# Layer 1's first feed-forward product by seven quarter products in a two-layer attention trunk

## The chip, the cores and the metric

The kernel runs on one NeuronCore of a Trainium2 chip. The engines named here are TensorE (PE in the profile, with PEld for its weight loads), VectorE (DVE), ScalarE (ACT), GpSimd (POOL) and SyncE (SP), which issues the DMAs. The metric is the device time of one execution in microseconds.

## The reference

Two layers of a diffusion trunk work on 512 latent tokens and 256 context tokens of width 1024. Each layer is attention in two branches, an output projection, and a SwiGLU feed-forward. Cut to what the change touches:

```python
D_MODEL, SEQ, DEPTH, CTX_LEN = 1024, 512, 2, 256
D_FF = 2816
def swiglu(h, w_in, w_out):
    a, u = jnp.split(h @ w_in, 2, axis=-1)
    return (jax.nn.silu(a) * u) @ w_out
for l in range(DEPTH):
    ...
    x = x + g1 * branch_merge(ya, yb, ga, gb, w_pa[l], w_pb[l], w_o[l])
    ...
    h2 = modulate(rms_norm(x, norm2[l]), sh2, sc2)
    x = x + g2 * swiglu(h2, w_ffn_in[l], w_ffn_out[l])
    ...
return rms_norm(x, final_norm)
```

The context goes through the feed-forward in layer 0 only, so the feed-forward has 768 tokens in layer 0 and 512 in layer 1.

## The kernel before

Activations lie with channels on the 128 partitions and tokens along the free dimension. The width is 8 blocks of 128 channels (KB = 8), the hidden width 22 blocks (FB = 22). TensorE works on fp32 in a rounded form, so each operand is split into a high part, made by a ScalarE copy, and a low part, made by a subtraction. A product of two operands is then three matmuls: high x high, high x low, low x high. The weight of a block comes by DMA into a raw tile (`wr`, four buffers) and is split into `wh` and `wl` (three buffers each). The subtraction runs on GpSimd, or on VectorE where `weight` is given `nc.vector` (line 361).

The instruction order of TensorE is written out by hand where the code says `manual_schedule`. Elsewhere, and on the other engines, the framework's scheduler sets the order; each engine runs its instructions in that fixed order.

The first product of a feed-forward makes, for each hidden block f, an a-part and a u-part: 128 hidden channels each, over 1024 input channels.

Layer 0 (`ffn`, 768 tokens in halves of nh = 384) makes blocks 0 and 1 plainly, half by half, because the norm of the second half is still under way. The generator `late` does that norm and is advanced by a running sum of matmul costs. All other blocks go by seven products of quarters. The 2x2 quarters of the left side are a- and u-part by lower and upper half of the input channels; those of the right side are lower and upper input channels by first and second half of the tokens. `Quarters` forms the four sums of weights on VectorE (lines 1925 to 1930) and splits each of the seven left factors (`split`, lines 1472 and 1473). `out_proj` and `late` form and split the right factors B11, B21, B12, B22 and T1 to T4 (`cut`, lines 1547 and 1548; `sums`). `quad` issues the seven products into three PSUM banks u, c, v (names qu, qc, qv, line 1580). A ScalarE copy (line 1587) takes the running sum of bank u out after the first, the third and the fifth product. `Hidden` finishes the block: line 1960 adds u3 to bank v, line 1945 adds in silu, line 1947 multiplies, line 1965 and line 1969 multiply by the u-part. `ended` splits the finished block. `weave` puts the first product of the next block ahead of a block's last two. After blocks 5, 9, 13 and 17 `outputs` runs the second product over the next four finished blocks and adds it to x (`residual`, line 1447). The last six blocks' second product runs at the end by groups of tokens, with the sum of squares for the next norm. The conditioning reductions of the list `beside` (52 calls, lines 441 and 443, VectorE) are spread over this stage of layer 0.

Layer 1 (`ffn_plain`, 512 tokens) makes every block plainly: per block and part, 8 input blocks x 3 matmuls of 512 columns. The blocks are taken in chunks of 6, 6, 6 and 4, each followed by its second product. Blocks 0 to 2 run in two token halves of 256 columns, five parts in the first half ahead of any in the second (`ahead`), while the norm of the second half is made by the generator `norm`. From block 3 on, and in the second product, the weights' low parts are made by GpSimd. The last chunk's second product runs for tokens 0 to 255, then 256 to 511, each followed by the final norm and store (`final`).

The output projection ahead of it (`out_proj_plain`) runs in the same two token halves. After the first half it modulates the eight blocks (`modulate`, lines 528 to 530): VectorE writes a scratch tile u, ScalarE adds the shift and writes the high part, VectorE writes the low part. Tiles named acc, sq and u come from the 45 common slots there.

Of the kernel before, what the change touches and what calls it, by code (L numbers as in the profile page):

```python
# [12 lines left out]
F32 = mybir.dt.float32  # L13
F32R = mybir.dt.float32r
# [6 lines left out]
P = 128  # L21
# [13 lines left out]

CHUNKS = ((0, 6), (6, 6), (12, 6), (18, 4))
# [20 lines left out]
EARLY, TEMPS = 2, 4  # L57
# [267 lines left out]
class Trunk:  # L325
# [176 lines left out]

    def norm(self, l, i, x, acc, a, b, h, pool):

        yield NORM[l][0]
        st = self.rstd(acc, b - a, pool, True)
        yield NORM[l][1]
        rb = self.spread(st, (b - a) // P, pool)
        for k in range(KB):
            self.modulate(l, i, k, x, rb, a, b, h, pool)  # L510
# [940 lines left out]
    def out_proj_plain(self, l, merged, x, groups, pool, beside):  # L1451
        h2 = ([], [])
        for a, b in groups:
            acc = None
            for j in range(KB):
                w = self.weight(self.d["wo"][l, j], D, self.nc.vector)
                if beside:
                    beside.pop(0)()
                ps = self.ps("a", "po")[:, : b - a]
                self.gemm(ps, w, merged, a, b)  # L1460
                self.residual(l, 0, ps, x, j, a, b)
                acc = self.square(x[j], a, b, pool, acc)
            if b == groups[-1][1]:
                return h2, lambda pool: self.norm(l, 1, x, acc, a, b, h2, pool)
            self.modulated(l, 1, x, acc, a, b, h2, pool)

# [9 lines left out]
    def out_proj(self, l, merged, x, nh, pool, beside):  # L1476
# [3 lines left out]
        for half in range(2):  # L1480
# [10 lines left out]
            if half == 0:  # L1491
                self.mod_bias(l, 24, 40)
                self.derive(l, 1)
                rb = self.rstd(acc, nh, pool)
                for k in range(KB):
                    self.modulate_half(l, k, x, rb, 0, nh, hf)
                    right.setdefault(("B11", "B21")[k >= KB // 2], []).append(
                        self.cut(hf[k][:, :nh], nh, self.slot, self.nc.vector))
        return right, lambda pool: self.late(l, x, acc, nh, hf, right, pool)

    def late(self, l, x, acc, nh, hf, right, pool):
# [7 lines left out]
        spare = lambda n, dt: pool.tile([P, T], dt, tag="ps", name=self.name(n))  # L1509
# [118 lines left out]
    def ffn(self, l, right, late, x, spans, groups, nh, done, pool, beside):  # L1628
# [4 lines left out]
        spans = groups  # L1633

        def slot(f, n):
            return pool.tile([P, T], F32R, tag="ps", name=self.name(n)) if f % 2 else self.slot(n, F32R)
# [10 lines left out]
        def whole(f, up, half):  # L1647
            if (f, up) not in weights:
                weights[f, up] = self.weight(d["wfi"][l, 2 * f + up], D, nc.vector)
                if not up:  # L1650
                    raws[f] = self.slot("ph")
# [12 lines left out]
        def ended(f):  # L1664
            ph, src = second.setdefault(min(f, FB - LAST) // CHUNK, ([], [])), raws[f][:, : 2 * nh]
            hi, lo = slot(f, "ph"), slot(f, "pl")
            nc.scalar.activation(hi, src, AF.Copy)
            nc.vector.tensor_tensor(lo, src, hi[:].bitcast(F32), op=ALU.subtract)
# [12 lines left out]
        def rest():  # L1681
            for f in range(EARLY, FB):
# [3 lines left out]

        clock, due = 0.0, next(late)
        with self.tc.manual_schedule(engines={mybir.EngineType.PE}):
            for f, up, half in (
                (0, 0, 0), (0, 1, 0), (1, 0, 0), (0, 0, 1), (0, 1, 1), (1, 0, 1), (1, 1, 0), (1, 1, 1)):  # L1690
# [19 lines left out]
        for a, b in groups:  # L1710
            acc = None
            for j in range(KB):
# [4 lines left out]
                acc = self.square(x[j], a, b, pool, acc)  # L1717
            done(acc, a, b)

    def ffn_plain(self, l, h2, late, x, spans, groups, done, pool, beside):  # L1720
        nc, d = self.nc, self.d
        for c0, c in CHUNKS:
            ph = ([], [])
            weights, ts = {}, {}

            def part(f, up, a, b):
                if (f, up) not in weights:
                    weights[f, up] = self.weight(
                        d["wfi"][l, 2 * f + up], D, nc.vector if f < 3 else None, pool if f == 0 else None)
                    if up:  # L1730
                        hi, lo = self.slot("ph", F32R), self.slot("pl", F32R)
                        ph[0].append(hi)
                        ph[1].append(lo)
                    else:
                        ts[f] = pool.tile([P, T], F32, tag="qt", name=self.name("t"))
                t = ts[f]
                ps = self.ps("a", "pf")[:, : b - a]
                yield from self.steps(ps, weights[f, up], h2, a, b)
                if not up:
                    nc.scalar.activation(t[:, a:b], ps, AF.Tanh, scale=0.5)  # L1740
                    nc.vector.scalar_tensor_tensor(t[:, a:b], t[:, a:b], 1.0, ps, op0=ALU.add, op1=ALU.mult)
                else:
                    hi, lo = ph[0][f - c0], ph[1][f - c0]
                    nc.vector.tensor_tensor(t[:, a:b], t[:, a:b], ps, op=ALU.mult)
                    nc.scalar.activation(hi[:, a:b], t[:, a:b], AF.Copy)
                    nc.vector.tensor_tensor(lo[:, a:b], t[:, a:b], hi[:, a:b].bitcast(F32), op=ALU.subtract)

            first = c0
            if c0 == 0:

                first = 3
                clock, due = 0.0, next(late)
                with self.tc.manual_schedule(engines={mybir.EngineType.PE}):
                    ahead = [(0, 0), (0, 1), (1, 0), (1, 1), (2, 0)]
                    for f, up, g in (
                        *((f, up, 0) for f, up in ahead), *((f, up, 1) for f, up in ahead), (2, 1, 0), (2, 1, 1)):
                        for cost in part(f, up, *groups[g]):
                            clock += cost
                            if due is not None and clock > due:
                                due = next(late, None)  # L1760
            for f in range(first, c0 + c):
                for up in range(2):
                    for a, b in spans:
                        drain(part(f, up, a, b))
            end = c0 + c == FB
            if end:
                for a, b in groups:
                    acc = None
                    for j in range(0, KB, 2):
                        w = self.weight(d["wfo"][l, j : j + 2, :, c0 * P : (c0 + c) * P], 2 * c * P)  # L1770
                        for i in range(2):
                            ps = self.ps("a", "po")[:, : b - a]
                            drain(self.steps(ps, w, ph, a, b, c, i * c))
                            self.residual(l, 1, ps, x, j + i, a, b)
                            if l == DEPTH - 1 and b == groups[-1][1] and j + i >= KB - 2:

                                acc = [acc] if j + i == KB - 2 else acc
                                acc.append(pool.tile([P, S], F32, tag="sq", name=self.name("sq")))
                                nc.scalar.activation(acc[-1][:, : b - a], x[j + i][:, a:b], AF.Square)
# [156 lines left out]
class Hidden:  # L1936
# [34 lines left out]
    def done(self):  # L1971
        self.ended(self.f)
# [110 lines left out]
```

## Time and profile before

| what | value |
|---|---|
| median of 3 runs | 2014.64 us (2013.2 to 2015.53) |
| the profiled execution | 2013.65 us, of which the span is 2011.8 us |
| mean granted TensorE clock | 0.982 of full speed |
| TensorE busy | 1947.7 us, 11516 matmuls |
| VectorE busy | 1382.1 us |
| ScalarE busy | 889.5 us |
| GpSimd busy | 450.0 us |
| layer 1's feed-forward, from the first matmul of its blocks alone to the end of the span | 1629 to 2011.8 us |

Times in rows are counted from the start of the span. Busy times of TensorE overlap, as matmuls are pipelined: the step from one matmul's start to the next is what counts, not the duration in its row. Likewise a VectorE row's duration reaches some 0.1 us into the next operation when the engine is busy, so the step from start to start is its price.

### The profile page before, as it was taken

How to read it: one execution, taken by the hardware profiler on the slowest of the kernel's cores; microseconds unless marked ns; L12 is line 12 of the kernel's file. 1: busy time of each engine (PE TensorE's matmuls, PEld its weight loads, DVE VectorE, ACT ScalarE, POOL GpSimd, SP SyncE). 2: the span in 40 equal slices, each digit the busy share in tenths (PEclk: the TensorE clock that was granted, in tenths of full speed). 3: DMA queues.
4: the chain of work that ended last, by engine and by line, in shares of the span. 5: the costliest groups of instructions: out<-in, count | busy, mean ns of one | idle time of the engine just before them, and what ended most of it. 6: DMA issues, size and time to landing. Idle time of an engine off the chain costs nothing. (4 is left out here: it accounts for less than half of the span.)

```text
span 2011.8 us, 29695 instructions
## 1 busy us (share of the span) xinstructions
PE 1947.7 (97%) x11516; PEld 1767.4 (88%) x11516; DVE 1382.1 (69%) x2498; ACT 889.5 (44%) x1646; POOL 450.0 (22%) x236
## 2 busy tenths in 40 slices
PE   7999999999989999999999989999999999999998
PEld 7898999988889999889899878889988998888887
DVE  7577888779787998888857576888654563232326
ACT  4466666552235533333334345666553442222224
POOL 5522213213300000000000014332322003534444
PEclk7899999999999999999999989999999999999999
DMA  7211112234464244456422432112233532323233
GB/s 287 65 55 50 38 53 87 64 112 161 136 246 143 67 134 135 142 162 202 134 82 61 125 111 64 56 48 64 77 89 110 195 110 87 113 76 118 79 115 95
DMA packets 73405, 218.61 MB, mean 109 GB/s; under 512 B 8624, under 2 KB 10800, under 8 KB 73264
## 3 DMA queue, kind: packets, MB, share of 16 engines
q1 hardware_dynamic: 73264, 216.71, 34.2%
q8 instruction: 91, 1.49, 0.3%
q14 instruction: 50, 0.41, 0.1%
HBM read 204.62 MB, written 6.82 MB: 105 GB/s over the span
## 5 line engine op out<-in xcount | busy, mean ns | idle before, releaser
L361 POOL TENSOR_TENSOR wl<-wr,wh 128x1024 fp32r<-128x1024 f32 (+2 forms) x156 | 330.7, 2124 | 713.7 <-ACT wh L359 684.4
L359 ACT ACTIVATE wh<-wr 128x1024 fp32r<-128x1024 f32 (+2 forms) x257 | 235.5, 919 | 547.2 <-issue 197.1
L374 PE MATMUL pj<-h,wh 128*128 128x512 f32 (+1 forms) x720 | 262.5, 367 | 4.0 <-DVE mb L1437 1.5
L374 PE MATMUL pj<-hl,wh 128*128 128x512 f32 (+1 forms) x720 | 254.4, 354 | 3.1 <-DVE hl L530 3.1
L374 PE MATMUL pj<-h,wl 128*128 128x512 f32 (+1 forms) x720 | 254.2, 353 | 0.0
L374 PE MATMUL po<-ph,wh 128*128 128x512 f32 (+1 forms) x560 | 193.2, 347 | 0.0
L374 PE MATMUL po<-pl,wh 128*128 128x512 f32 (+1 forms) x560 | 192.8, 345 | 0.0
L374 PE MATMUL po<-ph,wl 128*128 128x512 f32 (+1 forms) x560 | 191.3, 345 | 0.0
L1580 PE MATMUL qu<-r,w 128*128 128x384 f32 x960 | 175.3, 335 | 1.8 <-ACT tt L1587 1.8
L1580 PEld LDWEIGHTS qu<-r,w 128*128 128x128 f32 x960 | 166.7, 188 | 4.0 <-ACT tt L1587 3.9
L1447 DVE SCALAR_TENSOR_TENSOR x<-po,G,x 128x256 f32<-128x256 f32 (+3 forms) x160 | 91.9, 588 | 113.3 <-PE po L374 113.0
L496 POOL TENSOR_TENSOR rs<-rs,expo 128x2 f32<-128x2 f32 (+2 forms) x8 | 6.2, 772 | 678.6 <-DVE rs L495 678.6
L374 PEld LDWEIGHTS pj<-h,wh 128*128 128x128 f32 x720 | 137.6, 191 | 19.3 <-DVE mb L1437 1.8
L374 PEld LDWEIGHTS pj<-hl,wh 128*128 128x128 f32 x720 | 137.7, 191 | 18.1 <-DVE hl L530 4.0
L374 PEld LDWEIGHTS pj<-h,wl 128*128 128x128 f32 x720 | 137.2, 191 | 18.6
L374 PE MATMUL pf<-h,wh 128*128 128x512 f32 (+1 forms) x400 | 146.8, 367 | 1.0 <-ACT h L529 1.0
L374 PE MATMUL pf<-hl,wh 128*128 128x512 f32 (+1 forms) x400 | 146.7, 367 | 1.1 <-DVE hl L530 0.9
L374 PE MATMUL pf<-h,wl 128*128 128x512 f32 (+1 forms) x400 | 146.3, 366 | 0.0
L1007 ACT ACTIVATE pth<-tp 128x512 fp32r<-128x512 f32 x176 | 103.5, 596 | 65.9 <-PE tp L1057 37.4
L1008 DVE TENSOR_TENSOR ptl<-tp,pth 128x512 fp32r<-128x512 f32 x176 | 119.8, 685 | 14.2 <-ACT pth L1007 12.5
L374 PEld LDWEIGHTS po<-ph,wh 128*128 128x128 f32 x560 | 105.7, 189 | 14.1 <-ACT wh L359 1.1
L374 PEld LDWEIGHTS po<-pl,wh 128*128 128x128 f32 x560 | 105.8, 189 | 13.0
(243 smaller groups left out, 4524.3 us busy)
## 6 DMA issues: line engine op xcount, KB each, us to landing
wr<-wmodT SPq DMA_DIRECT2D x91, 512.0 KB, 3.8
wr<-wfi SPq DMA_DIRECT2D x88, 512.0 KB, 3.6
wr<-win SPq DMA_DIRECT2D x68, 512.0 KB, 3.6
wr<-wo SPq DMA_DIRECT2D x32, 512.0 KB, 4.3
wr<-wfo SPq DMA_DIRECT2D x40, 384.0 KB, 3.1
wr<-wp SPq DMA_DIRECT2D x32, 256.0 KB, 2.6
wr<-wfo SPq DMA_DIRECT2D x32, 256.0 KB, 2.7
x<-x SPq DMA_DIRECT2D x16, 384.0 KB, 7.6
```

The costliest lines, as they stand in the source:

```text
L359: nc.scalar.activation(hi, raw, AF.Copy)
L361: (eng or nc.gpsimd).tensor_tensor(lo, raw, hi[:].bitcast(F32), op=ALU.subtract)
L374: nc.tensor.matmul(ps[:, : b - a], u[:, c], v[k][:, a:b], start=(k == 0 and i == 0), stop=(k == nk - 1 and i == 2),)
L496: nc.gpsimd.tensor_tensor(r[:, :nb], r[:, :nb], self.expo[:, :nb], op=ALU.pow)
L1007: nc.scalar.activation(hi, tp, AF.Copy)
L1008: nc.vector.tensor_tensor(lo, tp, hi[:].bitcast(F32), op=ALU.subtract)
L1447: self.nc.vector.scalar_tensor_tensor(x[j][:, f:u], ps[:, f - a : u - a], self.G[l][i][:, s, j : j + 1], x[j][:, f:u], op0=ALU.mult, op1=A ...
L1580: nc.tensor.matmul(banks[bank], u[:, c], v, start=(first and k == 0 and i == 0), stop=(k == kn - 1 and i == 2), skip_group_check=True)
```

## The change

Layer 1 now uses `out_proj`, `late` and `ffn` as layer 0 does, with nh = 256. `out_proj_plain`, `norm` and `ffn_plain` are gone. Three blocks go plainly ahead in layer 1: five parts in the first half of the tokens, the same five in the second half, then the sixth part in both (`EARLY`, `COVER`). For layer 0 these lists give the old order. Blocks 3 to 21 go by quarters, with all low parts on VectorE. The second product's chunks become 4, 4, 4, 4 and 6. The tiles of the pool "ps" shrink to the tokens in use. Block 0's plain weights keep their own four tiles ("we"). The last two columns' squares stay separate summands for the final norm, as before. The core of the diff:

```diff
-CHUNKS = ((0, 6), (6, 6), (12, 6), (18, 4))
-EARLY, TEMPS = 2, 4
+EARLY = [((0, 0), (0, 1), (1, 0), (1, 1)), ((0, 0), (0, 1), (1, 0), (1, 1), (2, 0), (2, 1))]
+COVER = 3, 5
+TEMPS = 4
...
-    def norm(self, l, i, x, acc, a, b, h, pool):
-    def out_proj_plain(self, l, merged, x, groups, pool, beside):
-    def ffn_plain(self, l, h2, late, x, spans, groups, done, pool, beside):
...
             if half == 0:
-                self.mod_bias(l, 24, 40)
-                self.derive(l, 1)
+                if l == 0:
+                    self.mod_bias(0, 24, 40)
+                    self.derive(0, 1)
...
-        spare = lambda n, dt: pool.tile([P, T], dt, tag="ps", name=self.name(n))
+        spare = lambda n, dt: pool.tile([P, 2 * nh], dt, tag="ps", name=self.name(n))
...
-        spans = groups
...
-                weights[f, up] = self.weight(d["wfi"][l, 2 * f + up], D, nc.vector)
+                weights[f, up] = self.weight(
+                    d["wfi"][l, 2 * f + up], D, nc.vector, pool if "we" in pool.bufs and f == 0 else None)
...
-            for f in range(EARLY, FB):
+            for f in range(len(early) // 2, FB):
...
+        early, cover = EARLY[l], COVER[l]
+        order = [(*part, half) for half in range(2) for part in early[:cover]]
+        order += [(*part, half) for part in early[cover:] for half in range(2)]
...
-                acc = self.square(x[j], a, b, pool, acc)
+                if l == DEPTH - 1 and b == groups[-1][1] and j >= KB - 2:
+                    acc = [acc] if j == KB - 2 else acc
+                    acc.append(pool.tile([P, S], F32, tag="sq", name=self.name("sq")))
+                    nc.scalar.activation(acc[-1][:, : b - a], x[j][:, a:b], AF.Square)
+                else:
+                    acc = self.square(x[j], a, b, pool, acc)
...
-                        project = self.out_proj_plain if last else self.out_proj
-                        right, late = project(l, merged, x, groups if last else nh, pool, beside)
+                        right, late = self.out_proj(l, merged, x, nh, pool, beside)
...
-                        own = dict(acc=2, sq=2, u=2, qt=4, we=4) if last else dict(ws=1, tt=TEMPS, ps=7)
-                        pool = _Bufs(pool_, dict(own, rs=2), None if last else slots)
+                        own = dict(we=4) if last else {}
+                        pool = _Bufs(pool_, dict(own, ws=1, tt=TEMPS, ps=7, rs=2), slots)
...
-                        if last:
-                            self.ffn_plain(l, right, late(pool), x, spans, groups, final, pool, beside)
-                        else:
-                            self.ffn(l, right, late, x, spans, groups, nh, following, pool, beside)
+                        self.ffn(
+                            l, right, late, x, spans, groups, nh, final if last else following, pool, beside)
```

More of the change, by code (lines that the diff above doesn't have):

```diff
@@ L501, in spread @@
         return rb
-    def norm(self, l, i, x, acc, a, b, h, pool):
[L505 to L510, printed above, removed]
     def modulated(self, l, i, x, acc, a, b, h, pool):
@@ L1449, in residual @@
                 op0=ALU.mult, op1=ALU.add)
-    def out_proj_plain(self, l, merged, x, groups, pool, beside):
[L1452 to L1461, printed above, removed]
-                acc = self.square(x[j], a, b, pool, acc)
-            if b == groups[-1][1]:
-                return h2, lambda pool: self.norm(l, 1, x, acc, a, b, h2, pool)
-            self.modulated(l, 1, x, acc, a, b, h2, pool)
     def split(self, src, n):
@@ L1632, in ffn @@
         late = late(pool)
-        spans = groups
         def slot(f, n):
-            return pool.tile([P, T], F32R, tag="ps", name=self.name(n)) if f % 2 else self.slot(n, F32R)
+            return pool.tile([P, 2 * nh], F32R, tag="ps", name=self.name(n)) if f % 2 else self.slot(n, F32R)
         def raw(f, up):
@@ L1666, in ended @@
             hi, lo = slot(f, "ph"), slot(f, "pl")
-            nc.scalar.activation(hi, src, AF.Copy)
-            nc.vector.tensor_tensor(lo, src, hi[:].bitcast(F32), op=ALU.subtract)
+            nc.scalar.activation(hi[:, : 2 * nh], src, AF.Copy)
+            nc.vector.tensor_tensor(lo[:, : 2 * nh], src, hi[:, : 2 * nh].bitcast(F32), op=ALU.subtract)
             ph[0].append(hi)
@@ L1685, in rest @@
                     yield FREE[1], outputs(f // CHUNK - 1)
+        early, cover = EARLY[l], COVER[l]
+        order = [(*part, half) for half in range(2) for part in early[:cover]]
+        order += [(*part, half) for part in early[cover:] for half in range(2)]
         clock, due = 0.0, next(late)
         with self.tc.manual_schedule(engines={mybir.EngineType.PE}):
-            for f, up, half in (
-                (0, 0, 0), (0, 1, 0), (1, 0, 0), (0, 0, 1), (0, 1, 1), (1, 0, 1), (1, 1, 0), (1, 1, 1)):
+            for f, up, half in order:
                 while half and len(right.get("B22", ())) < KB // 2:
@@ L1716, in ffn @@
                 self.residual(l, 1, ps, x, j, a, b)
-                acc = self.square(x[j], a, b, pool, acc)
-            done(acc, a, b)
-    def ffn_plain(self, l, h2, late, x, spans, groups, done, pool, beside):
[L1721 to L1733, printed above, removed]
-                    else:
[L1735 to L1779, printed above, removed]
-                            else:
-                                acc = self.square(x[j + i], a, b, pool, acc)
-                    done(acc, a, b)
-                break
-            for j in range(KB):
-                w = self.weight(d["wfo"][l, j, :, c0 * P : (c0 + c) * P], c * P)
-                for a, b in spans:
-                    ps = self.ps("a", "po")[:, : b - a]
-                    self.gemm(ps, w, ph, a, b, c)
-                    self.residual(l, 1, ps, x, j, a, b)
@@ L1891, in final @@
                                 nc.sync.dma_start(d["out"][k:up, :, a:b].rearrange("k p c -> p k c"), o)
-                        if last:
-                            self.ffn_plain(l, right, late(pool), x, spans, groups, final, pool, beside)
-                        else:
-                            self.ffn(l, right, late, x, spans, groups, nh, following, pool, beside)
+                        self.ffn(
+                            l, right, late, x, spans, groups, nh, final if last else following, pool, beside)
                     if not last:
```

## The prediction, made before the result

> **What bounds the kernel now.** I read the head of the page first, then the windows of layer 1's feed-forward stage, then the chain of waits there.
>
> ```profile
> span 2011.8 us, 29695 instructions
> PE 1947.7 (97%) x11516; PEld 1767.4 (88%) x11516; DVE 1382.1 (69%) x2498; ACT 889.5 (44%) x1646; POOL 450.0 (22%) x236
> ```
> ```profile
> core 0: us, PE busy (x) PEld busy (x) DVE busy (x) ACT busy (x) POOL busy (x), PEclk, DMA share, GB/s
> 1620.00:1640.00 20.00, 17.84 (x125) 16.63 (x124) 16.48 (x32) 10.53 (x20) 0.00 (x0) 0.91 0.57 184
> 1700.00:1750.00 50.00, 50.00 (x222) 41.42 (x222) 11.68 (x13) 12.03 (x14) 23.25 (x12) 1.00 0.37 109
> 1975.00:2000.00 25.00, 23.80 (x197) 23.47 (x195) 20.91 (x30) 17.03 (x35) 15.57 (x7) 1.00 0.19 61
> ```
> TensorE is the bound. Between 1700 and 1750 us it never idles at full clock, while VectorE works 11.68 of 50 us: in this stage TensorE time is span, and VectorE has room. The first and third rows are the places where it is not so: the start of the feed-forward (clock 0.91, 2.16 us idle) and its end.
>
> The chain of waits gives the price of a matmul.
>
> ```profile
> 1629.17 1.07 ACT wh L359
> ...
> 1643.95 8.74 PE pf L374 x73
> ...
> 1703.15 32.64 PE po L374 x144
> 1735.79 65.28 PE pf L374 x288
> ```
> 288 matmuls of 512 columns take 65.28 us, 0.2267 us each; 73 of 256 columns take 8.74 us, 0.1197 us each. Halving the columns does not halve the time: a straight line through both has 13 ns a matmul that do not shrink. This decides what seven products are worth.
>
> The Trainium skill, "TensorE: Matmul & The Clock Gate", section "Back-to-back issue gap", gives columns/2.4 + 2.5 ns, that is 0.2158 and 0.1092 us. By it the matmul terms below would come to -22.5 us (an estimate from that page); the trace shows a larger fixed part, so the measured rows are used.
>
> **The change, step by step.**
>
> *First product.* Each of the 22 blocks f was 2 x 8 x 3 = 48 matmuls of 512: 48 x 0.2267 = 10.88 us. A block by quarters is 7 products x 4 x 3 = 84 matmuls of 256: 84 x 0.1197 = 10.05; with 0.120, the step in the rows of the output projection, 10.08 us. It gains 0.80 us a block. Three blocks stay plain, in halves of 256 columns before and after alike (288 matmuls). So 19 x 0.80 = -15.2 us.
>
> *Second product.* Chunks 6, 6, 6, 4 become 4, 4, 4, 4, 6, and only the last runs in two halves of 256. Before: 18 x 24 x 0.2267 + 4 x 48 x 0.12 = 121.0; after: 16 x 24 x 0.2267 + 6 x 48 x 0.12 = 121.6. That is +0.6 us. Together: **-14.6 us** of TensorE time.
>
> *VectorE in the blocks.* GpSimd's subtractions move to it, and quarter sums are added. Per block: 4 sums and 7 splits of 512, one split of the result of 512, and 7 operations of 256 in the evacuations. Layer 0 does the same already, so the operations are in the trace (starts on a busy VectorE):
>
> ```profile
> 937.75 0.55 DVE L1945 TENSOR_TENSOR tt<-qv,tt 128x384 f32<-128x384 f32 x1
> 938.22 0.68 DVE L361 TENSOR_TENSOR wl<-wr,wh 128x512 fp32r<-128x512 f32 x1
> ...
> 942.18 0.48 DVE L1447 SCALAR_TENSOR_TENSOR x<-po,G,x 128x256 f32<-128x256 f32 x1
> 942.57 0.68 DVE L361 TENSOR_TENSOR wl<-wr,wh 128x512 fp32r<-128x512 f32 x1
> ...
> 960.43 0.69 DVE L361 TENSOR_TENSOR wl<-wr,wh 128x512 fp32r<-128x512 f32 x1
> 961.03 0.69 DVE L1926 TENSOR_TENSOR wr<-wr,wr 128x512 f32<-128x512 f32 x1
> ```
> From start to start, 512 columns cost 0.60 us, 384 cost 0.47, and 256 between 0.34 (the line through the two) and 0.39 (the L1447 row). A block costs 12 x 0.60 + 7 x 0.36 = **9.7 us of VectorE beside 10.08 of TensorE**: 96% full. Four blocks in a row leave 1.5 us of slack. Each chunk of outputs (8 x 0.60 split, 8 x 0.66 residual = 10.1 us beside 21.8) gives time back, and up to six split weight tiles may lie ahead. ScalarE: 8 x 0.6 + 5 x 0.4 = 6.8 us a block, free.
>
> So the means fit, and the price is in waits. Layer 0 is the nearest place, the same code at 384 columns:
>
> ```profile
> 683.64 2.24 PE L1580 MATMUL qu<-r,w 128*128 128x384 f32 x12
> 685.72 2.24 PE L1580 MATMUL qc<-r,w 128*128 128x384 f32 x12
> ...
> 750.73 0.40 PE L374 MATMUL po<-ph,wh 128*128 128x512 f32 x1
> ...
> 754.94 0.40 PE L374 MATMUL po<-ph,wh 128*128 128x512 f32 x1
> ...
> 1126.77 0.39 PE L374 MATMUL po<-ph,wh 128*128 128x512 f32 x1
> ```
> ```profile
> PE qv L1580 <- DVE tt L1960: 5.8, 5, 2.1
> PE qu L1580 <- ACT tt L1587: 1.8, 2, 1.1
> ```
> Its ideal: 20 blocks x 7 x 2.08 = 291.2, 32 output groups x 4.21 = 134.7, and 15 matmuls of the last chunk 3.5, in all 429.4 us; it took 1126.77 - 683.64 = 443.1. It lost 13.7 us, 0.68 a block, of which 7.6 are idle. Where?
>
> ```profile
> 833.85 1.22 DVE L441 CUSTOM_DVE_ANT_0 junk<-wr,crow 128x1024 f32<-128x1024 f32 x1
> 835.00 0.08 DVE L441 DVE_READ_ACCUMULATOR2_ANT mod<- 128x1 f32 x1
> 835.00 0.56 DVE L1960 TENSOR_TENSOR tt<-qv,tt 128x384 f32<-128x384 f32 x1
> 835.47 0.68 DVE L361 TENSOR_TENSOR wl<-wr,wh 128x512 fp32r<-128x512 f32 x1
> 835.61 3.52 PE L1580 MATMUL qv<-r,w 128*128 128x384 f32 x12 [1.80 <-DVE tt L1960]
> ```
> The evacuation at L1960 (TensorE may go on in that bank only after it) stood behind conditioning reductions of 1.22 us. Layer 1 has none of these. The stall also costs more than its idle time: the product behind it took 3.52 instead of 2.24 us. The skill's clock-gate page (section "What's actually happening") has the clock halve after an idle window of about 3.4 us; here 1.8 us idle slowed it, so a stall is priced at its idle time plus that. And where layer 0's VectorE was full but nothing stood in front, TensorE lost nothing:
>
> ```profile
> 680.00:700.00 20.00, 20.00 (x117) 20.00 (x116) 20.00 (x38) 10.26 (x19) 0.00 (x0) 1.00 0.21 58
> 700.00:720.00 20.00, 20.00 (x117) 20.00 (x116) 19.34 (x39) 9.55 (x18) 0.00 (x0) 1.00 0.40 130
> ```
> Bounds for the waits in layer 1's blocks: 0 (these rows) and 19 x 0.68 = +13.0. Against the low end: products are 1.44 us instead of 2.08, so an evacuation has 2.9 us of other products as cover rather than 4.2, a ScalarE copy 1.4. I take **+4 us**, nearer to the low end because the operations that caused layer 0's waits are missing.
>
> *The start.* From the first row below to the second, plus 4 matmuls done earlier, 288 matmuls took 41.3 + 0.5 us where 34.6 would do.
>
> ```profile
> 1629.05 0.28 PE L374 MATMUL pf<-hl,wh 128*128 128x256 f32 x1
> ...
> 1670.32 0.40 PE L374 MATMUL pf<-h,wh 128*128 128x512 f32 x1
> ```
> Of the 7.2 us lost, most lie before 1640: the modulated tiles came one by one, each through a scratch tile u of the common slots, with a 1.2 us weight split in between. The new code modulates in place and needs no u. It adds a second ScalarE pass per tile (8 x 0.4, ScalarE has room), and after the second norm 16 differences and 16 cuts of 256 columns, 32 x 0.34 = 10.9 us of VectorE. Those are needed only by the first quarter products, except the eight of B12 and B22. With weights (6 x 1.15), evacuations (4.4), modulation and cuts (5.9), result splits and block 3's sums (6), VectorE has some 34 us beside 34.6: no slack. Layer 0's start, built so, shows what that costs:
>
> ```profile
> PE pf L374 <- DVE r L1548: 1.6, 2, 1.1
> ```
> It was 39.2 us (644.5 to 683.64) for 192 x 0.1733 = 33.3 and 1.5 for the norm's own matmuls, 4.4 lost. Bounds: a gain of 5.9 (only the norm's matmuls remain) and a loss of 3.3 more than now (7.2 plus layer 0's stall at the second half). I take **-2 us**: layer 0's loss and a little for the fuller VectorE.
>
> *The end.* The last chunk's weight splits leave GpSimd.
>
> ```profile
> 1989.03 2.58 POOL L361 TENSOR_TENSOR wl<-wr,wh 128x1024 fp32r<-128x1024 f32 x1
> 1989.45 2.44 DVE L475 TENSOR_TENSOR acc<-acc,sq 128x256 f32<-128x256 f32 x1
> ```
> ```profile
> PE st L486 <- DVE acc L475: 1.2, 1, 1.2
> ```
> A VectorE addition of 256 columns takes 2.44 us while GpSimd subtracts, and TensorE waited 1.2 us for one. This goes. VectorE then has 0.9 (768-wide split) + 0.39 + 0.34 = 1.6 us per column block beside 18 x 0.12 = 2.16. The last block's result passes four operations (about 5 us in layer 0), covered by the other five k blocks of three or four j, 1.8 us each; uncovered it would cost up to 3. Bounds -2 to +3; I take **-1**. The final norm and store are untouched. DMA: a block loads 2 x 0.5 MB in 10 us, far under the rates seen; the SP queue issues as many loads, wfo in 16 pieces of 384 KB instead of 8 of 512 at the end. Priced at nothing: four raw tiles hold two blocks ahead; if a load came late, it would show as a wait for wr<-wfi at L1925.
>
> **Sum.** -14.6 + 4 - 2 - 1 = -13.6 us from the profiled 2013.65 (its span 2011.8 plus 1.85). The median of the runs, 2014.64, is 1 us above that execution, so I forecast **2001 us**. Measurement tells about 0.2%, 4 us.
>
> **Rivals.**
> 1. *Waits as in layer 0.* If the shorter products make waits as frequent as the reductions did, +13.0 in place of +4: -14.6 + 13 - 2 - 1 = -4.6, 2010 us. For it: the cover is a third shorter and VectorE 96% full. Against: every wait examined stood behind a reduction.
> 2. *VectorE becomes the bound* (the other side). If the order on VectorE leaves it idle now and then, or its operations cost their full shown durations, 12 x 0.69 + 7 x 0.42 = 11.2 us, each block lasts 11.2: 19 x 1.15 = 21.9 in place of 4, sum +4.3, 2019 us. It decides from 10.08 + 17.6/19 = 11.0 us of VectorE pace per block. Against: the 0.60 us steps, and the outputs in between, which this price leaves out.
> 3. *The gain isn't there* because the smaller matmuls run slower than 0.120 (clock or weight load). At 0.1295 a block is again 10.88. The output projection at clock 1.00 speaks against it; I fold it into rival 2.
>
> **Chances.** Forecast 0.62 (its own range 1995 to 2006), rival 1 0.23, half of it past 0.2% faster and a third within, rivals 2 and 3 0.15. Faster 0.75, same 0.10, slower 0.15. The range 1995 to 2012 leaves out rival 2 and the case of no waits with a start without loss (0.05).
>
> **What would show it.** In the new trace: 12 matmuls of qu, qv, qc at 1.44 us; blocks about 10.1 us apart; VectorE at nine tenths or more in the slices from 1670 to 1960 us; PE's waits for L1960, L1945 and the ScalarE copy L1587 of some 4 us in layer 1; no POOL rows of L361 there; the start between 1629 and block 3 near 40 us; additions at L475 of 0.4 us at the end. Wrong would be blocks at 11 us, a long wait for L1548 at the start, or a low granted clock throughout.

## The result, and the profile after

The changed kernel takes 1996.17 us (median of 4 runs, 1992.42 to 2001.58) beside 2015.09 us for the kernel before (4 runs, 2013.2 to 2016.9): a ratio of 0.9908, 95% interval 0.9883 to 0.9934. The forecast was 2001 us. The profiled execution took 1997.26 us where the one before took 2013.65, 16.4 us less. Measured again with more runs, the change was worth 19.9 us (experiment 1).

The head of the page after, then its windows at the start of layer 1's feed-forward, over 50 us of it, and over 26 of the 28 products of four blocks, a stretch without outputs (columns as in the windows of before):

```profile
span 1995.5 us, 31794 instructions
PE 1936.3 (97%) x12248; PEld 1789.7 (90%) x12248; DVE 1538.6 (77%) x2887; ACT 966.1 (48%) x1862; POOL 298.5 (15%) x166
```
```profile
1620.00:1640.00 20.00, 16.71 (x118) 15.61 (x117) 13.22 (x28) 8.64 (x20) 0.70 (x1) 0.91 0.37 126
1700.00:1750.00 50.00, 50.00 (x344) 46.40 (x343) 41.70 (x75) 24.32 (x49) 0.00 (x0) 1.00 0.32 103
1781.40:1818.80 37.40, 37.40 (x314) 37.40 (x313) 33.54 (x64) 23.25 (x47) 0.00 (x0) 1.00 0.29 87
```

TensorE issues 732 more matmuls in less time. VectorE, at 11.68 of 50 us before, now works 41.70 of 50, and 33.54 of 37.40 (90%) between two chunks of outputs; TensorE is busy in all of both windows. The first row cuts the start at another place than the row of before does, as the whole stage now begins 4 us earlier. Counted over 20 us from the end of the output projection, TensorE idles 3.3 us (1625 to 1645) beside 2.7 before (1629 to 1649): the start is no better. In both kernels the granted clock falls right behind these waits, to 0.66 of full speed over 5 us (1630 to 1635 after, 1634 to 1639 before). A matmul of 256 columns then takes 0.21 us instead of 0.12 for some 3.3 us, so the waits cost about 1.4 us more than their idle time (an estimate: 3.3 / 0.21 matmuls, 0.09 us each).

The chain of waits after shows the blocks and a chunk of outputs:

```profile
1666.02 1.44 PE qu L1557 x12
...
1718.69 1.44 PE qu L1557 x12
...
1756.10 0.69 PE po L375 x3
...
1759.76 21.65 PE po L375 x93
```

Twelve matmuls of a product take 1.44 us, 0.120 each. From 1718.69 to 1759.76, less the 0.69 of three output matmuls that slip in, four blocks take 40.38 us: 10.09 a block, where 10.08 was worked out. All of TensorE's waits from the output projection to the end (released by which operation; us in total, times, longest):

```profile
PE rb L500 <- POOL rs L497: 1.7, 2, 1.1
PE pf L375 <- DVE r L1525: 1.7, 2, 0.9
PE pf L375 <- ACT r L1524: 1.1, 2, 0.9
PE st L487 <- ACT sq L1700: 0.7, 1, 0.7
PE po L375 <- ACT wh L360: 0.6, 2, 0.4
PE po L375 <- DVE wl L362: 0.2, 1, 0.2
```

No product of quarters (qu, qc, qv) waits for anything in layer 1.

Where the span went. The stages are read from the first and last starts of tiles and from the chain; "start" runs from the end of the output projection to block 3, "blocks" from there to the last matmul of the second product, "tail" from there to the end.

| us | before | before again | after | after again |
|---|---|---|---|---|
| layer 0, first to last start of qu | 440.9 | 444.0 | 436.6 | 434.9 |
| layer 1, start | 41.42 | 41.36 | 41.05 | 41.11 |
| layer 1, blocks | 329.48 | 329.44 | 318.65 | 318.79 |
| layer 1, tail | 12.00 | 12.10 | 11.00 | 10.90 |
| span | 2011.8 | 2012.0 | 1995.5 | 1991.9 |

The three stages of layer 1 together give 382.9 us before and 370.7 after: **-12.2 us**, to a tenth the same in the second pair. In the two pairs 4.3 and 9.1 us more come from layer 0's stage, whose instructions and their order are the same in both kernels. The prediction had nothing there.

### The profile page after: what moved, and what is told of

The parts are those of the page before. It is cut to its first block, busy times and chain, and to the rows that moved or that the text cites. A ratio compares the mean times of both kernels' runs of the same rounds, so it can differ in the third digit from the quotient of the medians.

```text
span 1995.5 us, 31794 instructions
## 1 busy us (share of the span) xinstructions
PE 1936.3 (97%) x12248; PEld 1789.7 (90%) x12248; DVE 1538.6 (77%) x2887; ACT 966.1 (48%) x1862; POOL 298.5 (15%) x166
## 5 line engine op out<-in xcount | busy, mean ns | idle before, releaser
L360 ACT ACTIVATE wh<-wr 128x512 fp32r<-128x512 f32 (+2 forms) x235 | 200.2, 855 | 371.4 <-PE po L375 133.6
L1557 PE MATMUL qu<-r,w 128*128 128x384 f32 (+1 forms) x1872 | 294.8, 311 | 2.7 <-ACT tt L1564 2.6
L1557 PEld LDWEIGHTS qu<-r,w 128*128 128x128 f32 x1872 | 281.1, 189 | 6.9 <-ACT tt L1564 6.0
L362 POOL TENSOR_TENSOR wl<-wr,wh 128x1024 fp32r<-128x1024 f32 (+1 forms) x86 | 179.3, 2087 | 511.2 <-ACT wh L360 481.9
L1448 ACT ACTIVATE w<-wr 128x512 fp32r<-128x512 f32 x234 | 144.4, 628 | 127.7 <-PE po L375 26.3
L1449 DVE TENSOR_TENSOR w<-wr,w 128x512 fp32r<-128x512 f32 x234 | 159.0, 687 | 15.7 <-ACT w L1448 14.1
L362 DVE TENSOR_TENSOR wl<-wr,wh 128x512 fp32r<-128x512 f32 (+2 forms) x149 | 138.6, 933 | 20.3 <-ACT wh L360 19.0
L1557 PE MATMUL qv<-r,w 128*128 128x384 f32 (+1 forms) x936 | 150.9, 310 | 2.6 <-DVE tt L1871 2.6
L1439 DVE SCALAR_TENSOR_TENSOR x<-po,G,x 128x256 f32<-128x256 f32 (+3 forms) x168 | 98.1, 595 | 66.6 <-PE po L375 66.1
L1557 PEld LDWEIGHTS qv<-r,w 128*128 128x128 f32 x936 | 140.9, 189 | 3.5 <-DVE tt L1871 3.5
```

Source lines behind the costliest of these rows:

```text
L360: nc.scalar.activation(hi, raw, AF.Copy)
L362: (eng or nc.gpsimd).tensor_tensor(lo, raw, hi[:].bitcast(F32), op=ALU.subtract)
L1439: self.nc.vector.scalar_tensor_tensor(x[j][:, f:u], ps[:, f - a : u - a], self.G[l][i][:, s, j : j + 1], x[j][:, f:u], op0=ALU.mult, op1=A ...
L1448: nc.scalar.activation(t[:, :n], src, AF.Copy)
L1449: nc.vector.tensor_tensor(t[:, n : 2 * n], src, t[:, :n].bitcast(F32), op=ALU.subtract)
L1557: nc.tensor.matmul(banks[bank], u[:, c], v, start=(first and k == 0 and i == 0), stop=(k == kn - 1 and i == 2), skip_group_check=True)
```

## Experiments

**1. Both kernels again** (no edit), one beside the other.

> The changed kernel once more, unaltered. All engines' instruction streams are the same in both kernels up to layer 1's output projection, yet the changed kernel's profiled execution was already 4.1 us earlier there (first block matmul after the projection at 1625.0 against 1629.05 us). Theory A: that is chance between executions of layer 0's block stage, so the change itself is worth the 12.3 us seen after that point; this profile's layer 1 part (from the first block matmul after the projection to the end of the span) is again 370.5 +- 1 us, its layer 0 part may lie anywhere within some 5 us, and the timed gain comes out between 10 and 17 us. Theory B: the changed program is faster in layer 0 too; layer 0's part is again about 4 us shorter and the gain is 16 to 20 us.

> The kernel before, once more, for a second profile of it. Theory A: its layer 0 block stage (first quarter product to the first store of x, 452.3 us in the first profile against 448.0 in the changed kernel) comes out different from the first by up to some 5 us, while layer 1's part from the first block matmul after the projection to the end is 382.7 +- 1 us again. Theory B: the layer 0 stage is 452 +- 1 again.

The changed kernel took 1994.17 us (5 runs) beside 2014.09 (23 runs), ratio 0.9899 (0.9883 to 0.9915). The single run of the kernel before took 2013.79. The second and fourth columns of the table show that the division of the gain repeats: 12.1 us in layer 1, and layer 0's stage shorter again. For the changed kernel theory B came out: the gain is 19.9 us, and layer 0's part, measured as the texts above measure it (first quarter product to first store of x), is 446.3 us beside 455.4. For the kernel before theory A came out: 455.4 against 452.3 us, so one and the same program varies by 3 us there.

**2. Chunks of four alone, in the kernel before.**

```diff
-CHUNKS = ((0, 6), (6, 6), (12, 6), (18, 4))
+CHUNKS = ((0, 4), (4, 4), (8, 4), (12, 4), (16, 6))
...
-                    for j in range(0, KB, 2):
+                    for j in range(KB):
...
```

> The kernel before with one part of the change alone: layer 1's second product in chunks 4, 4, 4, 4, 6, the last by column block (weights 768 wide), all blocks still plain and GpSimd still used. By the sum of the prediction: +0.6 us. In the changed kernel, though, 96 matmuls of 512 columns of one chunk took 22.34 us, 0.2327 each, not 0.2267. If that step belongs to chunks of four (weight tiles of 512 columns), it shows here too, and the time is +2.9 us with 32 column blocks of 12 x 0.2327; if it belongs to the busy VectorE or the tiles of the changed kernel, the step here is 0.2267 and the time +0.6 us.

2013.44 us (12 runs), ratio 0.9994 (0.9984 to 1.0004): no difference that can be told, and not the +2.9 us of the first theory. Block 3 to the last matmul took 329.59 us beside 329.48, the tail 11.0 beside 12.0. The chain of this kernel has a chunk of outputs, all 96 matmuls, in one piece:

```profile
1682.28 21.79 PE po L374 x96
```

That is 0.2270 us a matmul. In the changed kernel the same 96 matmuls take 0.69 + 21.65 = 22.34 us, 0.2327 each. So neither the chunks nor their loads cost the difference; in these runs it appears only where the outputs stand among products of quarters, and layer 0's outputs show it as well. What slows them by 0.006 us each is not settled. VectorE's load alone is a weak candidate: in the kernel of experiment 5, where VectorE works 9.53 of 16.3 us beside layer 0's outputs instead of 20.01 of 22, the matmuls of 512 columns still take 0.233 us.

**3. GpSimd's subtractions of layer 1's feed-forward alone to VectorE, in the kernel before.**

```diff
-... nc.vector if f < 3 else None, pool if f == 0 else None)
+... nc.vector, pool if f == 0 else None)
...
-... c0 * P : (c0 + c) * P], 2 * c * P)
+... c0 * P : (c0 + c) * P], 2 * c * P, nc.vector)
```

> The kernel before with another part alone: layer 1's feed-forward makes all low parts on VectorE, no GpSimd there, everything else plain as before. VectorE then has about 2 x 1.15 us more per block of 10.9 us, TensorE stays the bound: nothing changes from 1670 to 1975 us; at the end the additions of 256 columns take 0.4 us instead of up to 2.4, and the 1.2 us wait for one goes: -1 to -2 us in all. Rival: the wait at the end goes but another takes its place (splits late on VectorE), 0 +- 1 us.

2012.9 us (12 runs), ratio 0.9992 (0.9981 to 1.0003). Blocks 1.4 us shorter, tail 0.8 longer. The 1.2 us for which TensorE waited for an addition is gone, as forecast, but what it gave is within the noise of the timing. Neither this nor the chunks are worth anything that can be measured by themselves. That leaves the quarter products for layer 1's 12 us, and their 10.09 us a block, read directly above, say the same.

**4. VectorE loaded further in the changed kernel.** Some of the subtractions that split the quarter weights are done twice, in layer 1 only: for two of seven factors (dve2, +1.2 us a block) and for all seven (dve7, +4.2 us).

```diff
-        nc.vector.tensor_tensor(t[:, n : 2 * n], src, ...)
+        for _ in range(1 + again):
+            nc.vector.tensor_tensor(t[:, n : 2 * n], src, ...)
...
```

> The changed kernel with VectorE loaded more: in layer 1's blocks the low parts of two of the seven left factors are subtracted twice (same result), 2 x 0.60 us a block, 10.9 us of VectorE beside 10.08 of TensorE. Theory A (VectorE may run ahead by up to six split tiles, 3.6 us, and wins back in each chunk of outputs): four blocks lack 3.1 us, which the lead covers; blocks stay at 10.08 us and the stage loses under 4 us in all. Theory B (whatever VectorE lacks per block shows in every block, as rival 2 of the prediction had it): 19 x 0.77 = 15 us more.

> The same with all seven low parts subtracted twice, 7 x 0.60 = 4.2 us more a block, 13.9 us beside 10.08. Theory A: each run of blocks between two chunks of outputs loses its lack less one lead, 19 x 3.8 - 5 x 3.6 = 54 us in all, with TensorE waiting in the blocks. Theory B: 19 x 3.8 = 72 us. Theory C (it averages over the whole stage): 19 x 13.9 + 4 x 10.1 = 304 us of VectorE beside 280 of TensorE, 24 us.

dve2 took 1999.06 us in a single run; its blocks 322.3 us, 3.6 more than the changed kernel's. dve7 took 2059.94, also once; its blocks 380.1, 61.4 more. TensorE's longest waits for VectorE in layer 1's quarter products, of dve2 and then of dve7:

```profile
PE qu L1558 <- DVE w L1450: 1.5, 2, 0.7
```
```profile
PE qu L1558 <- DVE w L1450: 41.4, 11, 6.7
PE qv L1558 <- DVE tt L1873: 3.2, 4, 1.1
```

By the prediction's count VectorE needs 9.7 us a block in the changed kernel, 10.9 in dve2 and 13.9 in dve7. At 10.9, past TensorE's 10.08, the excess would be 19 x 0.82 = 15.6 us; 3.6 of them show, so the rest is absorbed, and theory A (under 4 us) came out. At 13.9 the excess shows: 61.4 us lie between the 54 of theory A and the 72 of theory B (19 x 3.82), somewhat nearer to theory A, and far from the 24 of theory C. Of the 61.4, some 45 are idle time; the rest goes with a granted clock of 0.95 over these blocks, beside 1.00 in the changed kernel. Rival 2 was to decide from 11.0 us a block; the changed kernel, with blocks of 10.09 us and no wait in them, stays below.

**5. Layer 0's conditioning reductions left out of the changed kernel**, with their loads. The output is then not the reference's.

```diff
...
-                        first = [one(0, n) for n in range(44, 48)]
-                        first[-1] = lambda last=first[-1]: (last(), gate2())
+                        first = [gate2]
-                        beside += [(2.6 if n < 16 else 1.3, one(1, n)) for n in range(48)] + [(1.5, rest)]
+                        beside += [(1.5, rest)]
```

> The changed kernel without the 52 conditioning reductions and their loads in layer 0's blocks (the conditioning of layer 1 and part of layer 0's are left out, set to zero). Theory A (TensorE's waits in layer 0's blocks are evacuations standing behind these reductions): PE's waits for L1871 and L1564 go, and the stage from the first quarter product to the first store of x takes 439 +- 2 us instead of 446 to 448. Rival (they come from VectorE's and ScalarE's ordinary work on the blocks): over 444 us.

1987.89 us in a single run. In layer 0's block stage no wait of TensorE is left, and the stage shrinks from 436.6 us to 427.9 (by the measure of the text above, from 448.0 to 439.3, as theory A had it). TensorE's waits there in the changed kernel, which stand beside the two rows for layer 0 in the prediction:

```profile
PE qu L1557 <- ACT tt L1564: 2.6, 2, 2.0
PE qv L1557 <- DVE tt L1871: 2.6, 3, 1.0
```

So layer 0's waits come from the reductions with their loads; this run does not tell the two apart. That an evacuation stood right behind a reduction is what the row of 833.85 us in the prediction shows. Layer 1, which has none, does not wait in its blocks. Layer 0's stage can move without any change in its code: its waits are 7.6 us before and 5.2 after.

**6. The start: half of the output projection's low parts back to GpSimd.** In the changed kernel the second token half of the output projection runs beside modulation and cuts. I took VectorE's 1.2 us weight splits there for the cause of the late tiles.

```diff
-w = self.weight(self.d["wo"][l, j], D, self.nc.vector)
+w = self.weight(self.d["wo"][l, j], D, None if l and half else self.nc.vector)
```

> The changed kernel, with the weights' low parts of layer 1's output projection made by GpSimd again in its second token half (8 splits of 1024 columns). Theory A (the start of the feed-forward loses 7 us because VectorE, with two weight splits a column block beside the modulation, is late with the modulated tiles): VectorE has 1.15 us less per 2.88, the tiles are there in time, -3 to -5 us. Rival (a GpSimd subtraction holds up VectorE's additions and subtractions as at the end of the kernel before, 2.4 us instead of 0.4): 0 to +4 us.

1997.88 us (6 runs), ratio 0.9917 (0.9903 to 0.9931), and the start is 44.23 us, 3.2 longer. The groups of instructions between 1600 and 1630 us (count, then busy us and mean ns) show where VectorE's time goes, first in the changed kernel, then here:

```profile
L362 DVE TENSOR_TENSOR wl<-wr,wh 128x1024 fp32r<-128x1024 f32 x11 | 13.5, 1223 | 2.2 <-ACT wh L360 2.1
L1525 DVE TENSOR_TENSOR r<-hf,r 128x256 fp32r<-128x256 f32 x7 | 2.9, 420 | 0.0
```
```profile
L362 POOL TENSOR_TENSOR wl<-wr,wh 128x1024 fp32r<-128x1024 f32 x6 | 15.2, 2539 | 3.1 <-ACT wh L360 2.6 <-PE rb L500 0.5
L1525 DVE TENSOR_TENSOR r<-hf,r 128x256 fp32r<-128x256 f32 x8 | 7.6, 944 | 0.7 <-ACT r L1524 0.6
```

```profile
L1510 DVE SCALAR_TENSOR_TENSOR hf<-x,A,rb 128x256 f32<-128x256 f32 x8 | 3.7, 471 | 0.6 <-PE rb L500 0.6
```

While GpSimd subtracts, VectorE's cuts (L1525, both operands in SBUF, the engines' working memory) take 944 ns on average instead of 420; the modulation (L1510, last row, one operand, rb, in PSUM, where TensorE's results land) takes 471 beside 476. TensorE's wait for L1525 between 1560 and 1660 us rises from 1.7 to 3.9:

```profile
PE pf L375 <- DVE r L1525: 3.9, 3, 2.2
```

TensorE's idle time in the whole start grows by only 1.5 us, from 3.3 to 4.8. Part of the rest is slow matmuls: the steps of 0.21 us last 5.5 us here beside some 3.3.

The Trainium skill, "SBUF — State Buffer", section "SBUF: two separate sides", says that a VectorE operation with two SBUF inputs and a GpSimd operation that reads SBUF hold a shared pair of ports in turn, each for the whole instruction. The rows agree with it: 944 ns beside 420 for the cuts, 471 beside 476 for the modulation. My remedy failed: what the splits give back is lost in the cuts. That the splits set the start is an argument from the chain shown further down, not something this run shows.

**7. The last chunk's weights split earlier**, into the four tiles "we".

```diff
-                w = self.weight(d["wfo"][l, j, :, chunk * CHUNK * P :], LAST * P, nc.vector)
+                w = self.weight(d["wfo"][l, j, :, chunk * CHUNK * P :], LAST * P, nc.vector,
+                                pool if "we" in pool.bufs and a == 0 and j < 2 else None)
```

> The changed kernel, with the first two weights of the last chunk of outputs split into the spare weight tiles that the output projection has left free, so that more split weights lie ready when block 21's result comes. In the changed kernel TensorE lost about 2.9 us at the last chunk's start: its first column blocks waited for the splits (wh, wl 768 wide), which themselves waited for TensorE to give a split tile back. Theory T (tiles): the time from block 3 to the last matmul goes from 318.7 to about 316.5 us (316 to 317.5) and the row 'ACT wh L360 <- PE po' of the waits goes from 3.4 us to under 1.5. Rival V (order on VectorE: the splits stand behind block 21's evacuations whatever tile they have): 318.7 as now, within 0.5.

1995.25 us (5 runs), ratio 0.9912 (0.9896 to 0.9928); blocks 318.70 us, unchanged. More free tiles did not help, and the wait that theory T wanted shorter grew. Waits between 1936 and 1962 us, changed kernel first, then this one:

```profile
ACT wh L360 <- PE po L375: 3.4, 3, 1.3
```
```profile
ACT wh L360 <- PE po L375: 5.0, 3, 3.0
```

Theory T falls. That the order on VectorE holds the splits, as rival V says, fits the unchanged time but was not tried by itself.

**8. Two plain blocks ahead in layer 1 instead of three.**

```diff
-EARLY = [((0, 0), (0, 1), (1, 0), (1, 1)), ((0, 0), (0, 1), (1, 0), (1, 1), (2, 0), (2, 1))]
-COVER = 3, 5
+EARLY = [((0, 0), (0, 1), (1, 0), (1, 1)), ((0, 0), (0, 1), (1, 0), (1, 1))]
+COVER = 3, 4
```

> The changed kernel with two plain blocks in layer 1 instead of three, so that block 2 too goes by quarters, and four halves instead of five lie ahead of the second half's modulated tiles. Theory V (VectorE sets the start: in the second half of the output projection it has some 3.4 us for each column block beside 2.9 of TensorE): block 2's product gains 0.8 us, the start loses the cover of one half (2.9 us of TensorE work) of which about 2 show; start and blocks together, 359.8 us in the changed kernel, come out at 360.5 to 362, time +0.5 to +2.5 us. Rival C (the cover is not needed, tiles would come earlier because VectorE has two plain 1.2 us splits less): together 358.5 to 359.3, time -0.8 us.

1996.68 us (4 runs), ratio 0.9918 (0.9903 to 0.9934). Start and blocks together take 361.9 us beside 359.7: the cover lost costs more than the 0.8 us that the third block gains, and the sum lies in the 360.5 to 362 of theory V. That VectorE is why the cover is needed is the theory's reason; the run shows only the sum.

**9. Does the program's length move the loads?** Two forms of the kernel before, with instructions added on which nothing else depends. The first has 2100 one-column memsets on GpSimd, in the code ahead of layer 0's blocks; the second has, in the code behind the last store, 732 matmul passes, 389 memsets on VectorE and 216 copies on ScalarE, as many as the changed kernel has more.

```diff
+        for _ in range(2100):
+            nc.gpsimd.memset(self.idle, 0.0)
```
```diff
...
+                            for _ in range(366):
+                                nc.tensor.matmul(st[:, 0:1], self.ident, self.ones, start=True, stop=True)
+                            for _ in range(389):
+                                nc.vector.memset(self.idle[:, 0:1], 0.0)
+                            for _ in range(216):
+                                nc.scalar.activation(self.idle[:, 1:2], self.ones, AF.Copy)
```

> The kernel before, with 2100 memsets of one column on GpSimd where it is idle in layer 0's feed-forward, so that the program has as many instructions as the changed kernel (31,800 instead of 29,700); nothing waits for them. The question is why layer 0's blocks took 446 to 448 us in the changed kernel beside 452 to 455 before, with the same instructions, and 512 KB loads landed in 3.3 instead of 3.6 us all through. Theory P (the size of the program moves where its data or code lie): loads in 3.3 us (win) and layer 0's blocks 445 to 449, time about 2007. Rival N (not the size): 3.6 us and 451 to 456, time about 2014.

> The kernel before, with 366 norm-sized matmuls (732 passes), 389 one-column memsets on VectorE and 216 one-column copies on ScalarE appended behind its last store, so that each of these engines has as many instructions as in the changed kernel. The added work comes after everything else and lengthens the span by some 50 to 150 us; what is read is layer 0, which is the same as before. 2100 instructions added on GpSimd alone had moved nothing (loads of win in 3.6 us, layer 0's blocks 452.9 us). Theory P2 (the length of these engines' programs moves the loads): win lands in 3.3 us and layer 0's blocks take 445 to 449. Rival N (something else in the program): 3.6 us and 451 to 456.

The first took 2020.89 us and the second 2165.55, each in a single run. The traces show that most of the added work did not run where the two texts above put it (operation, count; after the colon its duration in ns, then its first and last start in us). The first form, then the second:

```profile
L1636 POOL MEMSET idle<- x2100: 88/98/780, 0.7 to 522.9; 128x1 f32 x191
```
```profile
L1900 DVE MEMSET idle<- x389: 59/59/59, 0.9 to 164.2; 128x1 f32 x195
L1902 ACT ACTIVATE idle<-ones x216: 183/203/231, 2.0 to 125.7; 128x1 f32<-128x1 f32 x108
L1898 PE MATMUL st<-ones,ident_sb x732: 212/352/353, 2006.4 to 2162.2; 128*128 128x1 f32 x183
```

As nothing orders them, the memsets and the copies were scheduled at the start of the program; only the matmuls ran at its end. None of the added work ran in layer 0's block stage, but in both forms this stage begins later than in any other kernel here (691.0 and 687.5 us, beside 678.5 to 684.6), and the first form's total says nothing of the loads.

The loads of one weight (count, size, median us from issue to landing) show this line in the kernel before, and the same line with GpSimd padded:

```profile
wr<-win SPq DMA_DIRECT2D x68, 512.0 KB, 3.6
```

In the changed kernel, and in the kernel before with the other three engines padded, it is this:

```profile
wr<-win SPq DMA_DIRECT2D x68, 512.0 KB, 3.3
```

The 88 loads of wfi (512 KB) go the same way, 3.6, 3.6, 3.3 and 3.3 us; the 32 of wo, of the same size, do not (4.3, 4.4, 4.4 and 4.3). And the first and last start of qu in layer 0, GpSimd padded, then the other three engines padded:

```profile
L1581 PE MATMUL qu<-r,w x960: 333/334/448, 691.0 to 1132.6; 128*128 128x384 f32 x192
```
```profile
L1581 PE MATMUL qu<-r,w x960: 333/334/445, 687.5 to 1125.1; 128*128 128x384 f32 x192
```

That is 441.6 and 437.6 us, beside 440.9 before and 436.6 after. By the measure of the expectations the stage takes 452.9 and 449.0 us, the second at the upper edge of theory P2's 445 to 449. Over all profiles, the five of the kernel before and its variants, without the second padding, lie at 440.7 to 444.0 us with win landing in 3.6 us; the seven of the changed kernel and its variants that leave layer 0 alone lie at 433.0 to 438.2 with 3.2 or 3.3 us. The second padding puts the kernel before among the latter, though no added work runs in this stage; the first does not. So the part of the gain that lies in layer 0 (about 6 us, the difference of the two groups' means, 441.7 and 435.7) may go with the length of the programs of TensorE, VectorE and ScalarE, and not with what they compute. This is not shown: it rests on one profile, and that kernel differs from the other not only in length but also in the work that VectorE and ScalarE do in the first 164 us. How the loads would land sooner stays open, and so does how sooner landing would shorten the stage, since VectorE's own waits for the reductions' loads there hardly differ (20.4 us in all before, 19.6 after).

## Why the prediction came out as it did

The time lies 5 us under the forecast and inside the forecast's own range. Term by term it is less tidy.

**Products, -15.2:** right. 19 x (10.88 - 10.09) = -15.0 us. Rival 3 is out: the matmuls ran at 0.120. The -22.5 us that the prediction sets beside its own sum comes from a formula that the Trainium skill, "TensorE: Matmul & The Clock Gate", section "Back-to-back issue gap", gives for a single, isolated matmul, not for a stream of weight loads and matmuls as here; the measured rows were the right choice.

**Second product, +0.6:** mis-sized. It took 0.2267 us for the 384 matmuls of 512 columns in the four chunks of four; they took 0.2327, 2.3 us more, +2.9 in all. The step that failed was to carry a duration from one stretch of the kernel to another; layer 0's outputs, in the trace of before, already ran at 0.233.

**Waits in the blocks, +4:** none. The low bound was right, and the reason given for staying near it (layer 0's waits come from its reductions) is what experiment 5 shows. I left +4 for VectorE at 96%; in experiment 4 even an excess of 0.8 us a block cost only 3.6 of 15.6 us. That the outputs between the blocks give the rest back fits both runs there, but was not tried by itself. Rival 1 falls because no quarter product of layer 1 waits, and rival 2 because the blocks take 10.09 us.

**The start, -2:** it gave 0.3. The step that failed is the cause named for the loss before, the scratch tile u: the prediction took u off the path and priced VectorE's added work there by its amount, not by its place on the path. The chain of waits before, from the last weight split to the point from which TensorE runs on, goes twice through u:

```profile
1630.27 1.23 DVE wl L361
1631.49 0.40 DVE hl L530
1631.89 0.40 DVE u L528
...
1632.32 0.52 ACT h L529
...
1632.86 0.48 DVE hl L530
1633.34 0.40 DVE u L528
...
1633.77 0.52 ACT h L529
...
1634.31 0.50 DVE hl L530
...
1634.85 7.03 PE pf L374 x44
```

And after:

```profile
1626.11 1.23 DVE wl L362
1627.33 0.39 DVE hf L1510
1627.72 0.20 DVE r L1525
...
1627.98 0.68 DVE ws L1836
1628.66 0.39 DVE hf L1510
1629.05 0.60 DVE wr L1837
1629.65 0.35 DVE r L1525
...
1630.04 7.52 PE pf L375 x47
```

From the end of the split it is 3.36 us before and 2.71 after. Two of block 3's weight sums (L1836, L1837) stand on the chain with 1.28 us, although block 3's first product at 1666.02 needs them only some 37 us later. Without them the chain would have given about 1.9 us, near the 2 that were forecast (an estimate from these rows; an order with the sums later was not tried). The weight split itself stands on both chains. So the record shows the order of VectorE's queue on the path; that it alone sets the pace of the start is not shown.

**The end, -1:** the tail gave 1.0 (12.0 to 11.0), with the additions now at 0.42 us as predicted:

```profile
L476 DVE TENSOR_TENSOR acc<-acc,sq x7: 416/418/422, 1957.7 to 1968.4; 128x256 f32<-128x256 f32 x7
```

The reason is doubtful, though: without GpSimd's subtractions (experiment 3) TensorE's 1.2 us wait for an addition went, and with it 1.4 us of the blocks, but the tail of the kernel before grew to 12.8; with a last chunk of six blocks (experiment 2) the tail was 11.0, with GpSimd still at work. So the tail's 1.0 goes with the last chunk, not with GpSimd. And that chunk's start, called covered, lost more than the old one. In the chain:

```profile
1950.23 0.96 DVE wl L362
1951.23 2.17 PE po L375 x16
...
1955.14 0.96 DVE wl L362
1956.14 15.34 PE po L375 x126
```

From block 3 to the last matmul the matmuls alone come to 327.7 us before (19 x 10.88 + 121.0) and 315.6 after (19 x 10.09 + 384 x 0.2327 + 288 x 0.12, the outputs of the last chunk in two halves). Measured were 329.5 and 318.65: 1.8 us of waits and slowed matmuls before, 3.0 after. So the end as a whole is about +0.2 instead of -1.

**Sum.** -15.0 + 2.9 + 0 - 0.3 + 0.2 = -12.2 us, as the stages show, against -13.6 predicted: the waits that did not come paid for the slower outputs and the start that gave nothing. The rest of the gain, some 7 us, is mostly layer 0's, which no step of the prediction had; without layer 0's 6 us the time would have been about 2002 us. So the forecast came out right in part by luck: of its terms the quarter products held, and the errors of the others nearly cancelled.

Of the signs named in advance, the 1.44 us, the 10.1 us blocks, VectorE at nine tenths in the blocks (0.83 with outputs), no GpSimd rows in the blocks and the 0.4 us additions came; the 4 us of waits and the start near 40 us did not.

## What to carry to other kernels

Price a smaller product by the step of its own shape in the trace, and take the steps of the unchanged neighbours from a stretch that already looks like the new one. Here an engine filled to 96% beside the bound cost nothing in a stretch where slack recurs; what stood on the chain of waits was a long operation, or one not yet needed, ahead of one that TensorE waited for. Instructions on which nothing depends may run far from where the code has them, so look in the trace where a control's added work ran before reading anything from it. Before a gain is credited to a change, compare the stages that it does not touch: here about a third of it lay in one of those.

## What the runs showed of the hardware that was not expected

Loads of the weights win and wfi (512 KB) landed in 3.2 or 3.3 us in the changed kernel, in its variants, and in the kernel before with 732 matmul passes, 389 memsets on VectorE and 216 copies on ScalarE added. They landed in 3.5 to 3.7 us in the kernel before and its other variants, among them the one with 2100 more instructions on GpSimd. Loads of wo, of the same size, took 4.2 to 4.4 us in both groups. Why is open.

Matmuls of 512 columns took 0.2327 us among products of quarters and 0.2267 to 0.2270 elsewhere, at full granted clock in both. Why is open.

Four waits of TensorE in the start of layer 1, 2.7 us in all within 5 us, were followed by 3.3 us of matmuls at 0.21 us instead of 0.12, with a granted clock of 0.66.

A VectorE subtraction of 256 columns took 944 ns on average while GpSimd subtracted and 420 ns otherwise, but the modulation of 256 columns, with one operand in PSUM, took 0.47 us in both.
